# One bias buffer for both halves of a convolution, and three projection panels one stage earlier, in a decoder layer

## The chip, the core and the metric

The kernel runs on one core of a Trainium2 chip. A core has four engines that compute and take their work from queues of their own: TensorE (PE) multiplies matrices into PSUM, VectorE (DVE) and ScalarE (ACT) work elementwise, GpSimd (POOL) does small things. SyncE (SP) issues nearly all DMAs here. What counts is the device time of one execution, in microseconds (us). The inputs, weights and intermediate results that don't fit lie in DRAM.

## What is computed

One layer of a decoder on 1024 tokens of width 1024: a mixer made of a convolution group and a recurrent group, cross-attention into 256 memory tokens, and a gated feed-forward; each with a norm before and after, and a residual. Cut to what matters here:

```python
h = rms_norm(x, g[0])
p = h @ w_in_first                                  # 1024 columns for the convolution, 1792 for the recurrence
y_conv = conformer_conv(p[..., :2 * D_CONV], ...)
y_rwkv, _ = rwkv7_mix(p[..., 2 * D_CONV:], ...)
x = x + rms_norm(jnp.concatenate([y_conv, y_rwkv], -1) @ w_out, g[1])
x = x + rms_norm(memory_cross_attention(rms_norm(x, g[2]), ...), g[3])
x = x + rms_norm(swiglu(rms_norm(x, g[4]), ...), g[5])

def conformer_conv(u, conv_w, conv_b, ln_g, ln_b):
    h = u[..., :D_CONV] * sigmoid(u[..., D_CONV:])
    h = depthwise_causal_conv(h, conv_w) + conv_b   # 31 taps on each of 512 channels
    return silu(layer_norm(h, ln_g, ln_b))
```

## The kernel before

**Halves.** The sequence is worked off in two halves of 512 tokens (`b` is 0 or 1). Everything of half 1 up to its recurrence depends on half 0 only through small state, so that work of both halves can run side by side.

**Projections.** A matrix product in float32 is made of three with split operands: `split` writes a rounded copy (`hi`, on ACT) and the rest (`lo`, on DVE); `mm3` multiplies three pairs. `wload` loads 512 KB of weights (`wraw`, four buffers) and splits them into `whi` and `wlo` (two buffers each). `feat` is one projection of 128 columns for 512 tokens: 24 matmuls into `psf`. `w_in_block` runs panels, pairs of such projections; the input projection has 22 of them for each half: 8 for the convolution (`conv_cols`, stored in `hd`) and 14 for the recurrence (`mix_cols`, seven panels, stored in `pdr`; `evq` and `carry` are their evacuation on DVE).

**The convolution.** `conv_taps` loads 128 channels (`hin`), starts the sum with an ACT operation that multiplies by the first tap and adds the bias, and adds 30 taps on DVE (`acc`); 4 groups of channels make 120 taps for a half. `conv_norm` sums the groups (`lnsa`, `lnsb`), lets PE sum over channels with a matrix of ones (`psln`), and goes through squares, a reciprocal square root, and a SiLU whose two ACT operations read scale and bias. The result goes to DRAM (`yd`).

**The stages around the change.** While the recurrence of half 0 (`rwkv_chain`, tiles `Sn`, `Y`, `psp` to `psy`) runs, `weave` interleaves the memory products and the convolution projections of half 1 (`main`) with the convolution of half 0 in the program. The rest of half 1's input projection is a `filler`: 14 projections that `fill` takes a few at a time wherever the program has a gap. Then `mix_out(0)` loads `yd` (`araw`), splits it and multiplies with `w_out` into `pst`; `residual` adds and norms four token tiles (`ya`) and PE transposes them (`pstr`); `attention(0)` multiplies with `gd`, does a softmax and multiplies with `vwd`, then a second `residual`. The convolution of half 1 (`conv(1, kp)`) is woven into these two. Behind them come the feed-forward of half 0, as filler for the recurrence of half 1, and then half 1's own stages.

**Order.** The program order is not the order on the engines: when the program is built, a scheduler that estimates times puts every instruction in its engine's queue as soon as its inputs and buffers allow. Buffers (`bufs`) thus decide what may run ahead. Inside a queue the order is fixed.

## Time and profile before

| | us |
|---|---|
| median of 3 runs | 1670.16 (1668.98 to 1670.85) |
| the profiled execution | 1666.79 |
| its span, first to last instruction | 1665.1 |
| PE busy in it | 1513.3 |
| DVE busy in it | 1068.6 |
| ACT busy in it | 686.9 |

A profile lists what each engine did in one execution. Busy time as a share of the span tells which engine is full on average; windows tell it for a stretch; the list of waits tells for whom an engine stood still; the timeline gives each instruction with its start. Matmuls overlap, so that their own durations are longer than the step from one to the next.

### The profile page before, as it was taken

The page shows a single profiled execution, that of the slowest core. Times are in us where ns is not written, and L with a number is a line of the kernel's source. Part 1 is how long each engine was busy: PE and PEld are TensorE (multiplying, and loading weights), DVE is VectorE, ACT ScalarE, POOL GpSimd, SP SyncE. Part 2 cuts the span into 40 slices and gives each one's busy share as a digit, 9 for nine tenths or more (in the row PEclk, how much of TensorE's full clock was granted, in tenths as well). Part 3 has the DMA queues.
Part 4 walks back from the last instruction along what each step waited for, and adds up shares of the span by engine and source line. Part 5 has one row for each costly group of instructions (what it writes and reads, how often), then busy time and mean ns, then how long its engine had stood idle before and what let it go on. Part 6 is the DMA issues. An engine that isn't in the chain of part 4 may idle for free.

```text
span 1665.1 us, 22614 instructions
## 1 busy us (share of the span) xinstructions
PE 1513.3 (91%) x8688; PEld 1239.4 (74%) x8688; DVE 1068.6 (64%) x1702; ACT 686.9 (41%) x1062; POOL 50.8 (3%) x102
## 2 busy tenths in 40 slices
PE   7999879995009899999999999999999999999997
PEld 6787768874007688878788877888888788888886
DVE  5678676899998745568868355556446734444345
ACT  5654455543133634465522343444334432222222
POOL 1000100000000100100000000001001100000000
PEclk9999889998559999999999999999999999999999
DMA  5577996763014722645685544356226732332321
GB/s 206 170 223 213 310 304 191 240 201 101 6 35 155 253 76 95 201 141 174 181 230 189 153 149 148 111 167 210 81 89 203 252 102 89 101 101 89 102 89 51
DMA packets 175643, 257.36 MB, mean 155 GB/s; under 512 B 68912, under 2 KB 110000, under 8 KB 175536
## 3 DMA queue, kind: packets, MB, share of 16 engines
q1 hardware_dynamic: 174576, 255.08, 48.2%
q8 instruction: 68, 1.11, 0.3%
q10 hardware_dynamic: 960, 0.85, 0.2%
q14 instruction: 39, 0.32, 0.1%
HBM read 196.58 MB, written 59.31 MB: 154 GB/s over the span
## 4 chain that ended last, share of the span: by engine, by line
PE 81%; DVE 11%; DMA 4%; ACT 3%; issue 1%; SPq 0%; POOL 0%; DVEq 0%; POOLq 0%; ACTq 0%
PE psf L190 14%; PE psf L192 14%; PE psf L191 14%; PE pst L190 10%; PE pst L191 10%; PE pst L192 10%; DVE acc L342 6%; PE psg L514 1%; DVE wlo L168 1%; PE pstr L270 1%; PE pspr L428 1%; DMA gd<-evg 1%; ACT whi L167 1%; DMA xt<-in_x_dram 1%; DMA hin<-hd 1%
## 5 line engine op out<-in xcount | busy, mean ns | idle before, releaser
L168 DVE TENSOR_TENSOR wlo<-wraw,whi 128x1024 fp32r<-128x1024 f32 x256 | 312.8, 1223 | 321.7 <-ACT whi L167 319.7
L167 ACT CAST whi<-wraw 128x1024 fp32r<-128x1024 f32 x256 | 268.2, 1049 | 548.8 <-PE psf L191 228.7
L190 PE MATMUL psf<-ahi,whi 128*128 128x512 f32 (+1 forms) x1200 | 455.6, 381 | 3.2 <-ACT whi L167 3.0
L192 PE MATMUL psf<-ahi,wlo 128*128 128x512 f32 (+1 forms) x1200 | 454.9, 380 | 2.1 <-DVE wlo L168 2.1
L191 PE MATMUL psf<-alo,whi 128*128 128x512 f32 (+1 forms) x1200 | 454.7, 379 | 0.0
L190 PEld LDWEIGHTS psf<-ahi,whi 128*128 128x128 f32 x1200 | 227.7, 190 | 47.2 <-ACT whi L167 4.8
L192 PEld LDWEIGHTS psf<-ahi,wlo 128*128 128x128 f32 x1200 | 227.5, 190 | 44.9 <-DVE wlo L168 3.0
L191 PEld LDWEIGHTS psf<-alo,whi 128*128 128x128 f32 x1200 | 227.8, 190 | 42.3 <-issue 1.2
L342 DVE SCALAR_TENSOR_TENSOR acc<-hin,cols,acc 128x512 f32<-128x512 f32 x240 | 166.9, 746 | 4.0 <-ACT acc L340 3.8
L190 PE MATMUL pst<-whi,ahi 128*128 128x512 f32 x384 | 138.6, 400 | 22.7 <-ACT ahi L167 21.6
L191 PE MATMUL pst<-wlo,ahi 128*128 128x512 f32 x384 | 150.7, 394 | 0.0
L192 PE MATMUL pst<-whi,alo 128*128 128x512 f32 x384 | 147.3, 394 | 0.0
L191 PE MATMUL pst<-wlo,fhi 128*128 128x512 f32 x352 | 137.9, 392 | 0.0
L190 PE MATMUL pst<-whi,fhi 128*128 128x512 f32 x352 | 134.2, 392 | 0.0
L192 PE MATMUL pst<-whi,flo 128*128 128x512 f32 x352 | 134.1, 390 | 0.0
L190 PEld LDWEIGHTS pst<-whi,ahi 128*128 128x128 f32 x384 | 72.7, 191 | 40.1 <-ACT ahi L167 23.1
L191 PEld LDWEIGHTS pst<-wlo,ahi 128*128 128x128 f32 x384 | 73.1, 190 | 14.9
L192 PEld LDWEIGHTS pst<-whi,alo 128*128 128x128 f32 x384 | 72.2, 189 | 15.1 <-DVE alo L168 0.2
L903 DVE TENSOR_TENSOR ya<-pst,ya 128x512 f32<-128x512 f32 x80 | 54.2, 688 | 43.7 <-PE pst L192 43.5
L921 DVE SCALAR_TENSOR_TENSOR ftg<-ftg,psf 128x512 f32<-128x512 f32 x44 | 30.2, 685 | 76.4 <-PE psf L192 76.1
L191 PEld LDWEIGHTS pst<-wlo,fhi 128*128 128x128 f32 x352 | 66.1, 188 | 14.2 <-DVE wlo L168 0.4
L192 PEld LDWEIGHTS pst<-whi,flo 128*128 128x128 f32 x352 | 66.1, 188 | 13.6
(236 smaller groups left out, 1664.3 us busy)
## 6 DMA issues: line engine op xcount, KB each, us to landing
wraw<-in_w_gu_dram SPq DMA_DIRECT2D x88, 512.0 KB, 3.6
wraw<-in_w_in_dram SPq DMA_DIRECT2D x44, 512.0 KB, 4.1
wraw<-in_w_down_dram SPq DMA_DIRECT2D x44, 512.0 KB, 3.5
wraw<-in_wkv_dram SPq DMA_DIRECT2D x16, 512.0 KB, 5.7
am<-amd SPq DMA_DIRECT2D x16, 512.0 KB, 4.4
wraw<-in_w_out_dram SPq DMA_DIRECT2D x16, 512.0 KB, 3.7
wraw<-gd SPq DMA_DIRECT2D x16, 512.0 KB, 4.5
wraw<-vwd SPq DMA_DIRECT2D x16, 512.0 KB, 3.3
```

The source lines that it names most:

```text
L167: self.nc.scalar.copy(out=hi, in_=src)
L168: self.nc.vector.tensor_tensor(out=lo, in0=src, in1=hi.bitcast(F32), op=ALU.subtract)
L190: mm(ps, w[0], x[0], start=start, stop=False)
L191: mm(ps, w[0], x[1], start=False, stop=False)
L192: mm(ps, w[1], x[0], start=False, stop=stop)
L270: nc.tensor.transpose(ps[:, t * P:(t + 1) * P], xt[:, k * P:(k + 1) * P], self.ident)
L342: nc.vector.scalar_tensor_tensor(out=a, in0=h[:, k:k + TB], scalar=w(k), in1=a, op0=ALU.mult, op1=ALU.add)
L428: nc.tensor.matmul(ps, w, x, start=i == 0, stop=i == len(terms) - 1)
L514: nc.tensor.matmul(pg[g][:, i, :], bk[half[g], c + i, :], aq[half[g], :, c + i, :], start=True, stop=True)
L903: nc.vector.tensor_tensor(out=y, in0=ps, in1=y, op=ALU.add)
L921: nc.vector.scalar_tensor_tensor(out=tg, in0=tg, scalar=0.5, in1=pu, op0=ALU.mult, op1=ALU.mult)
```

## The change

Two things. First, the biases: the convolution bias (4 columns) and the layer norm's halved bias (4 columns) are copied into one tile `cb` of 8 columns, tag `convb`, which has one buffer. Half 0 reads the tile made at the start. When `conv_taps` begins for half 1, it allocates the tile anew in the same buffer and fills it with two ACT copies, which must wait until the last reader of half 0 has finished; all of half 1's sums start from it. A spare tile shrinks from 40 to 32 columns to make room. Second, the first three of the seven `mix_cols` panels of half 1 run in the `main` part of the recurrence's stage, and four are left to the filler; an empty `islice(w1, 0)` goes.

```diff
@@ -122,7 +122,7 @@
         nc.gpsimd.memset(self.mhalf, -0.5)
         self.carry = cp.tile([P, 14], F32, name="carry")
         nc.gpsimd.memset(self.carry, 0.0)
-        pad = cp.tile([P, 40], F32, name="pad")
+        pad = cp.tile([P, 32], F32, name="pad")
         nc.gpsimd.memset(pad, 0.0)
 
         def derive(name, n, src, mul, add):
@@ -139,6 +139,9 @@
         nc.vector.tensor_scalar(self.cwh, self.cwh, 0.5, None, op0=ALU.mult)
         self.lgh = derive("lgh", 4, col("ln_g"), 0.5, 0.0)
         self.lbh = derive("lbh", 4, col("ln_b"), 0.5, 0.0)
+        self.cb = cp.tile([P, 8], F32, tag="convb", name="convb0")
+        nc.vector.tensor_copy(out=self.cb[:, 0:4], in_=col("conv_b"))
+        nc.vector.tensor_copy(out=self.cb[:, 4:8], in_=self.lbh)
 
         self.hd = dr.tile([DR, CONVW - 1 + SEQ], F32, name="hd")
         self.pdr = dr.tile([14 * P, SEQ], F32, name="pdr")
@@ -331,13 +334,18 @@
 
     def conv_taps(self, b, pool, acc):
         nc = self.nc
+
+        if b == 1:
+            self.cb = self.cp.tile([P, 8], F32, tag="convb", name="convb")
+            nc.scalar.copy(out=self.cb[:, 0:4], in_=self.col("conv_b"))
+            nc.scalar.copy(out=self.cb[:, 4:8], in_=self.lbh)
         t0 = b * TB
         for j in range(4):
             h = pool.tile([P, 576], F32, tag="hin", bufs=2, name="hin")[:, 0:TB + CONVW - 1]
             nc.sync.dma_start(out=h, in_=self.hd[j * P:(j + 1) * P, t0:t0 + TB + CONVW - 1])
             a = acc[:, j, :]
             w = lambda k: self.cwh[:, j * CONVW + k:j * CONVW + k + 1]
-            nc.scalar.activation(out=a, in_=h[:, 0:TB], func=AF.Identity, scale=w(0), bias=self.col("conv_b", j))
+            nc.scalar.activation(out=a, in_=h[:, 0:TB], func=AF.Identity, scale=w(0), bias=self.cb[:, j:j + 1])
             for k in range(1, CONVW):
                 nc.vector.scalar_tensor_tensor(out=a, in0=h[:, k:k + TB], scalar=w(k), in1=a,
                                                op0=ALU.mult, op1=ALU.add)
@@ -377,7 +385,7 @@
             a = acc[:, j, :]
             nc.vector.tensor_tensor(out=a, in0=a, in1=ry, op=ALU.mult)
             th = pool.tile([P, TB], F32, tag="t", bufs=2, name="lnth")
-            sc, bi = self.lgh[:, j:j + 1], self.lbh[:, j:j + 1]
+            sc, bi = self.lgh[:, j:j + 1], self.cb[:, 4 + j:5 + j]
             nc.scalar.activation(out=th, in_=a, func=AF.Tanh, scale=sc, bias=bi)
             nc.scalar.activation(out=a, in_=a, func=AF.Identity, scale=sc, bias=bi)
             nc.vector.scalar_tensor_tensor(out=a, in0=th, scalar=1.0, in1=a, op0=ALU.add, op1=ALU.mult)
@@ -997,10 +1005,11 @@
                 yield 1.0 * 2
         maps = self.memory_maps(mT, ev, kv)
         w1 = self.w_in_block(1, h1, ev, conv_cols)
-        main = chain(islice(maps, 16), next_norm(), islice(w1, 0), maps, w1)
+        w1m = self.w_in_block(1, h1, ev, mix_cols[:3])
+        main = chain(islice(maps, 16), next_norm(), maps, w1, w1m)
         drain(weave(main, self.conv(0, kp), 1.0))
         pop("mix0", "gn0", "conv0", "tt0", "xb", "kv", "mk")
-        self.filler = self.w_in_block(1, h1, ev, mix_cols)
+        self.filler = self.w_in_block(1, h1, ev, mix_cols[3:])
 
         yp = push("y0", L)
         a2 = push("a2", L)
```

The engines' queues are built anew from that. Three places show it.

DVE in the recurrence's stage of half 0, before (`acc_2696` is half 0's sum, `acc_4446` half 1's, `Sn` the recurrence's state):

```order
L342 SCALAR_TENSOR_TENSOR acc_2696<-hin_3553,cols_77,acc_2696 128x512
L342 SCALAR_TENSOR_TENSOR acc_4446<-hin_4766,cols_77,acc_4446 128x512
L342 SCALAR_TENSOR_TENSOR acc_2696<-hin_3212,cols_77,acc_2696 128x512
L342 SCALAR_TENSOR_TENSOR acc_4446<-hin_4447,cols_77,acc_4446 128x512
L342 SCALAR_TENSOR_TENSOR acc_2696<-hin_3553,cols_77,acc_2696 128x512
L342 SCALAR_TENSOR_TENSOR acc_4446<-hin_4766,cols_77,acc_4446 128x512
L688 TENSOR_TENSOR Sn_2544<-pss_2535,Sn_2480 128x256
L342 SCALAR_TENSOR_TENSOR acc_2696<-hin_3212,cols_77,acc_2696 128x512
```

DVE at the same place, after (`acc_2699` is half 0's sum, `psf` and `evh` belong to half 1's convolution projections):

```order
L350 SCALAR_TENSOR_TENSOR acc_2699<-hin_3215,cols_77,acc_2699 128x512
L350 SCALAR_TENSOR_TENSOR acc_2699<-hin_3556,cols_77,acc_2699 128x512
L350 SCALAR_TENSOR_TENSOR acc_2699<-hin_3215,cols_77,acc_2699 128x512
L325 SCALAR_TENSOR_TENSOR evh_4307<-tg_4240,psf_4282 128x512
L350 SCALAR_TENSOR_TENSOR acc_2699<-hin_3556,cols_77,acc_2699 128x512
L350 SCALAR_TENSOR_TENSOR acc_2699<-hin_3215,cols_77,acc_2699 128x512
L171 TENSOR_TENSOR wlo_4351<-wraw_4348,whi_4350 128x1024
L696 TENSOR_TENSOR Sn_2547<-pss_2538,Sn_2483 128x256
L350 SCALAR_TENSOR_TENSOR acc_2699<-hin_3556,cols_77,acc_2699 128x512
L708 TENSOR_TENSOR Y_2561<-psy_2552,yq_2525 128x4x64
```

The taps of half 1 are gone from here; its first one now stands behind half 0's last step.

PE in front of the output projection, before (`psp` to `psbs` are the recurrence's last step, `pst` the output projection):

```order
L681 MATMUL psu_2605<-pt_2583,TT_1480 64x64 x8
L686 MATMUL pss_2616<-uv_2499,bt_2497 64x64
L696 MATMUL psy_2628<-am_2495,uv_2499 64x64
L686 MATMUL pss_2616<-uv_2499,bt_2497 64x64 x7
L696 MATMUL psy_2628<-am_2495,uv_2499 64x64 x7
L404 MATMUL psbs_2647<-yhl_2644,blk_105 128x512
L405 MATMUL psbs_2647<-yhl_2644,blk_105 128x512
L357 MATMUL psln_3824<-lnsa_3819,ones_86 128x512
L370 MATMUL psln2_3914<-lnsq_3911,ones_86 128x512
L190 MATMUL pst_4466<-whi_4472,ahi_4331 128x512
```

PE at the same place, after (`psf_4640` is the eighth of the 14 projections):

```order
L193 MATMUL psf_4640<-ahi_199,whi_4636 128x512
L194 MATMUL psf_4640<-alo_200,whi_4636 128x512
L195 MATMUL psf_4640<-ahi_199,wlo_4637 128x512
L365 MATMUL psln_3827<-lnsa_3822,ones_86 128x512
L378 MATMUL psln2_3917<-lnsq_3914,ones_86 128x512
L193 MATMUL pst_4694<-whi_4700,ahi_4559 128x512
```

Two of the 14 projections stood ahead of `psln` before; now eight do, and the recurrence's last step has moved ahead, among them.

DVE at the end of half 0's first residual, before (`ya_4458` and `ya_4459` are the third and fourth token tile, `evq` a projection's evacuation, `lnth` the end of half 1's convolution):

```order
L256 TENSOR_SCALAR ya_4458<-ya_4458,rstd_4899 128x1024
L304 SCALAR_TENSOR_TENSOR evq_4934<-psf_4909,cols_77,evq_4934 128x511
L307 SCALAR_TENSOR_TENSOR evq_4934<-carry_111,cols_77,evq_4934 128x1
L754 SCALAR_TENSOR_TENSOR ya_4459<-ya_4459,rstd_4942,xres_4940 128x1024
L383 SCALAR_TENSOR_TENSOR acc_4446<-lnth_6229,acc_4446 128x512
L309 COPY carry_111<-psf_4909 128x1
L229 TENSOR_SCALAR rstd_4950<-ss_4948 128x1
L168 TENSOR_TENSOR wlo_5106<-wraw_5103,whi_5105 128x1024
L304 SCALAR_TENSOR_TENSOR evq_4985<-psf_4960,cols_77,evq_4985 128x511
L307 SCALAR_TENSOR_TENSOR evq_4985<-carry_111,cols_77,evq_4985 128x1
L256 TENSOR_SCALAR ya_4459<-ya_4459,rstd_4950 128x1024
```

DVE at the same place, after (`ya_4686` and `ya_4687` are the third and fourth tile, `acc_4671` half 1's sum):

```order
L350 SCALAR_TENSOR_TENSOR acc_4671<-hin_5664,cols_77,acc_4671 128x512
L259 TENSOR_SCALAR ya_4686<-ya_4686,rstd_5127 128x1024
L350 SCALAR_TENSOR_TENSOR acc_4671<-hin_5467,cols_77,acc_4671 128x512
L762 SCALAR_TENSOR_TENSOR ya_4687<-ya_4687,rstd_5170,xres_5168 128x1024
L350 SCALAR_TENSOR_TENSOR acc_4671<-hin_5664,cols_77,acc_4671 128x512
L350 SCALAR_TENSOR_TENSOR acc_4671<-hin_5467,cols_77,acc_4671 128x512
L350 SCALAR_TENSOR_TENSOR acc_4671<-hin_5664,cols_77,acc_4671 128x512
L232 TENSOR_SCALAR rstd_5178<-ss_5176 128x1
L350 SCALAR_TENSOR_TENSOR acc_4671<-hin_5467,cols_77,acc_4671 128x512
L350 SCALAR_TENSOR_TENSOR acc_4671<-hin_5664,cols_77,acc_4671 128x512
L259 TENSOR_SCALAR ya_4687<-ya_4687,rstd_5178 128x1024
```

Before, half 1's taps were all ahead of this; now they stand between the steps of the tiles, by turns on two groups.

PE at half 0's second residual, before (`psf_6017` is the third of seven projections there, `pstr` the transposes of the first tile):

```order
L190 MATMUL psf_6017<-ahi_182,whi_6013 128x512
L191 MATMUL psf_6017<-alo_183,whi_6013 128x512
L270 MATMUL pstr_6172<-ident_81,ya_5560 128x128
L270 MATMUL pstr_6179<-ident_81,ya_5560 128x128
L270 MATMUL pstr_6186<-ident_81,ya_5560 128x128
L192 MATMUL psf_6017<-ahi_182,wlo_6014 128x512
```

PE at the same place, after (`psf_6157` is the only projection there):

```order
L194 MATMUL psf_6157<-alo_200,whi_6153 128x512
L195 MATMUL psf_6157<-ahi_199,wlo_6154 128x512
L273 MATMUL pstr_6252<-ident_81,ya_5788 128x128
L273 MATMUL pstr_6259<-ident_81,ya_5788 128x128
L273 MATMUL pstr_6266<-ident_81,ya_5788 128x128
```

Behind the transposes now follow the feed-forward's projections, which need their result; no other projection is left for this place.

## Rows read from the trace of the kernel before

**Rows 1.** the page's parts 1 and 2, shares of the span, and busy tenths by slice

```profile
PE 1513.3 (91%) x8688; PEld 1239.4 (74%) x8688; DVE 1068.6 (64%) x1702; ACT 686.9 (41%) x1062; POOL 50.8 (3%) x102
...
PE   7999879995009899999999999999999999999997
...
DVE  5678676899998745568868355556446734444345
```

**Rows 2.** windows: us, then busy us of PE, PEld, DVE, ACT, POOL, PEclk, DMA share, GB/s

```profile
400.00:501.00 101.00, 9.86 (x70) 5.41 (x70) 100.96 (x158) 22.05 (x31) 0.00 (x0) 0.52 0.10 34
501.00:560.00 59.00, 58.49 (x243) 47.36 (x244) 48.23 (x74) 29.23 (x49) 1.92 (x3) 0.95 0.52 173
560.00:580.00 20.00, 13.71 (x64) 10.90 (x63) 15.82 (x32) 12.99 (x20) 3.66 (x5) 0.88 0.84 311
...
680.00:728.00 48.00, 48.00 (x229) 39.87 (x228) 29.98 (x53) 21.86 (x33) 4.53 (x8) 1.00 0.65 202
```

**Rows 3.** waits of PE from 340 to 510: who waited for whom, us, times, longest

```profile
PE psln L357 <- DVE lnsa L351: 49.2, 1, 49.2
...
PE pst L190 <- ACT ahi L167: 21.6, 1, 21.6
```

**Rows 4.** timeline of DVE, 355 to 500: start, us, line, operation, tiles, count

```profile
356.52 0.68 DVE L351 TENSOR_TENSOR lnsa<-acc 128x512 f32<-128x512 f32 x1
...
396.99 1.21 DVE L168 TENSOR_TENSOR wlo<-wraw,whi 128x1024 fp32r<-128x1024 f32 x1
...
398.78 0.74 DVE L304 SCALAR_TENSOR_TENSOR evq<-psf,cols,evq 128x511 f32<-128x511 f32 x1
...
437.83 25.26 DVE L342 SCALAR_TENSOR_TENSOR acc<-hin,cols,acc 128x512 f32<-128x512 f32 x38
463.01 0.69 DVE L351 TENSOR_TENSOR lnsb<-acc 128x512 f32<-128x512 f32 x1
...
470.64 1.40 DVE L342 SCALAR_TENSOR_TENSOR acc<-hin,cols,acc 128x512 f32<-128x512 f32 x2
471.97 0.68 DVE L351 TENSOR_TENSOR lnsq<-lnsq 128x512 f32<-128x512 f32 x1
...
497.76 0.68 DVE L383 SCALAR_TENSOR_TENSOR acc<-lnth,acc 128x512 f32<-128x512 f32 x1
```

**Rows 5.** groups of DVE by line, 356 to 498.5: busy us, mean ns, idle before

```profile
L342 DVE SCALAR_TENSOR_TENSOR acc<-hin,cols,acc 128x512 f32<-128x512 f32 x154 | 105.9, 745 | 1.8 <-ACT acc L340 1.8
```

**Rows 6.** timeline of PE, 392 to 510

```profile
392.25 0.39 PE L192 MATMUL psf<-ahi,wlo 128*128 128x512 f32 x1
...
501.51 0.79 PE L190 MATMUL pst<-whi,ahi 128*128 128x512 f32 x1 [21.55 <-ACT ahi L167]
...
506.77 0.39 PE L190 MATMUL pst<-whi,ahi 128*128 128x512 f32 x1
```

**Rows 7.** the chain that ended last, around 354

```profile
353.63 5.14 DMA hin<-hd
```

**Rows 8.** timeline of ACT, 350 to 362

```profile
358.80 0.82 ACT L340 ACTIVATE acc<-hin,cols 128x512 f32<-128x512 f32 x1 [2.16 <-DMA hin<-hd]
```

**Rows 9.** timeline of PE at half 0's first residual

```profile
578.39 0.90 PE L270 MATMUL pstr<-ident,ya 128*128 128x128 f32 x3 [5.94 <-DVE ya L256]
579.64 0.80 PE L190 MATMUL pst<-whi,ahi 128*128 128x512 f32 x1 [0.35 <-ACT ahi L273]
```

**Rows 10.** timeline of DVE at half 0's second residual

```profile
678.72 1.27 DVE L754 SCALAR_TENSOR_TENSOR ya<-ya,rstd,xres 128x1024 f32<-128x1024 f32 x1
...
699.94 0.75 DVE L256 TENSOR_SCALAR ya<-ya,rstd 128x1024 f32<-128x1024 f32 x1 [0.60 <-POOL rstd L230]
```

**Rows 11.** timeline of PE at half 0's second residual

```profile
679.17 0.39 PE L192 MATMUL pst<-whi,alo 128*128 128x512 f32 x1
...
684.61 0.39 PE L192 MATMUL psf<-ahi,wlo 128*128 128x512 f32 x1
...
722.14 1.03 PE L270 MATMUL pstr<-ident,ya 128*128 128x128 f32 x8
```

## The prediction

> **What bounds the kernel now.** I read the busy tenths of the 40 slices first [rows 1]. TensorE (PE) is full nearly everywhere except in slices 10 to 12, and exactly there VectorE (DVE) is full. The windows give the sizes [rows 2]: from 400 to 501 us PE works 9.9 of 101 us at a granted clock of 0.52 (close to its lower level, 1.2 GHz) while DVE works 100.96. Behind it PE has no gap worth naming, but for 6.3 us in 560 to 580. So the kernel is PE-bound with one hole of about 100 us. The list of waits names what ends the hole [rows 3]: PE stands 49.2 us for `lnsa`, the sum over half 0's convolution, and 21.6 us for the first split input of the output projection, which reads that convolution's result.
>
> The timeline of DVE shows why half 0 is so late [rows 4]. Between `lnsa` at 356.5 and `lnsb` at 463.0 lie 106.5 us without a gap but 1.8 us [rows 5]. The order of before shows what runs there: 60 taps of half 0 and 59 of half 1, by turns. Half 1's result isn't read until the output projection of half 1, far behind; it takes the DVE time that half 0 needs at once.
>
> **Part 1, half 1 waits.** Both halves now read their biases from one buffer. Half 1's copy into it can't start before half 0's last activation has read it, and half 1's taps need that copy. The order of after has no tap of half 1 ahead of half 0's last step. A tap costs 25.26/38 = 0.665 us [rows 4]. Of the 106.5 us, 119 taps are 79.1 and all else 27.4. Without half 1: 60 taps, 39.9, and the 27.4. To this come six more projections (part 2). Each takes DVE a split of 1.21, an evacuation of 0.74 and two one-column steps; starts follow one another closer than the durations say (0.745 lasts a tap that takes 0.665 of the queue), so I take 2.0 a projection, 12.0 in all. The sum is 79.3, so `lnsb` starts at 356.5 + 79.3 = 435.8 in place of 463.0. PE doesn't set this end: it finishes its part of before at 392.6 [rows 6], the six projections add 32.7 (part 2), which makes 425.3, and the recurrence's small matmuls leave it some ten us of room.
>
> From `lnsb` to the output projection's first matmul were 38.5 us (463.0 to 501.51). Seven steps of that chain wait for one or two taps of half 1 in front of them, as the add at 471.97 does for the two taps at 470.64 [rows 4]; at about 1.2 each that is 8.2, which goes. It leaves 30.3, and the output projection starts at 466.1: **35.4 us earlier**. The layer norm's own latency stays bare, since DVE has nothing else queued in front of it now. The two bias copies on ScalarE (ACT) are 128x4, so between nothing and the 0.82 us of a 128x512 activation [rows 8] each; they stand behind half 0's last activation and cost half 0 nothing. The two at the start of the program hide behind the first loads.
>
> **Part 2, six projections move.** A projection is 24 matmuls; at full clock, 2.4 GHz, 24 in a row take 684.61 - 679.17 = 5.44 us [rows 11]. Before, two of the fourteen ran ahead of the hole's end; after, eight do. The six take 32.7 us of PE time out of the stretch behind, where PE is full (48.0 of 48 in 680 to 728 [rows 2]), and put them into the hole. Their loads, evacuations and stores go along on SP, ACT and DVE; ACT is busy 22 of 101 us there and the DMA share is 0.10. Parts 1 and 2 could give 35.4 + 32.7 = **68.1 us**, if nothing new were late.
>
> **Part 3, what is new at the first residual.** Now 120 taps, 79.8 us, must run beside the output projection and the first attention product, where 27 were left before. DVE was busy 48.2 of 59 us there [rows 2]. While the output projection runs this fits: its order puts 5 or 6 taps between two splits, 6 x 0.665 + 1.21 = 5.2 us, and PE needs 5.44 for what a split feeds. But the residual adds and scalings of the four token tiles stand between taps. From the first tap to the fourth scaling the order has 72 taps (47.9), 12 splits (13.7), 16 halves of 0.6 (9.6), 4 adds of 1.2, 4 scalings of 0.67, 4 evacuations with their columns (3.4) and small things: 84 us. The first tap starts near 463.3 (before, half 0's last step ended at 498.4 [rows 4], 3.1 us ahead of the projection's start). In the middle the last two groups' input must be loaded, with DVE waiting for it: such a load took 5.1 us and its activation 0.8 [rows 7, 8], and DVE has about 4.5 us of other work between the last tap on a group and the first on the next, so over both I add 3. The fourth scaling ends at 550.3, and the attention product follows 1.3 later [rows 9], at 551.6. That is 85.5 us after the output projection's start, against 579.64 - 501.51 = 78.1 before; the 5.9 us of waiting [rows 9] become 13 to 14. **Loss 7.4**, and 2 more for splits inside the product that come out a microsecond late. If DVE runs freely the loss is 0; if every tap in the way counts, see the rivals.
>
> **Part 4, the second residual loses its cover.** Before, seven projections ran between the last attention matmul at 679.17 and the last transposes at 722.14 [rows 11], 43.6 us without a gap. After, only one does, then PE waits for the four tiles. Their chain took from 678.72 to 699.94 plus 0.75 [rows 10], paced by the projections' own splits; the new order lets tiles three and four overlap, so I take 17 us from the last matmul. One projection covers 5.4, so PE waits 11.6; a restart at the lower clock costs 2.5 (12 matmuls took 506.77 - 501.51 = 5.26 [rows 6], at full clock half of 5.44), feeding the first projection 2, transposes 3.5 as before. Sum 25 for 43.6: of the 32.7 us only 18.2 arrive. **Loss 14.5.** If the chain were no shorter than before, 4 us more are lost; fully hidden, nothing.
>
> **Sum.** 68.1 - 7.4 - 2 - 14.5 = 44. The profiled execution took 1666.8, with a span of 1665.1; it would take 1623. The median of the runs is 3.4 above it, so I predict 1670.2 - 44 = **1626 us**.
>
> **Rivals.** *Everything is covered.* The taps let the residuals through and the feed-forward matmuls fill the second one: 68 off, 1602. For it: PE has always other matmuls in the program. Against: the order of PE puts the transposes ahead of them. *Only the panels count.* Something else ends the hole at 501 (the recurrence's output, also read by the projection): 18 off, 1652. Against: its last DVE step stands ahead of half 0's last taps in both orders. *Slower: the displaced taps land on PE's path.* DVE takes its work in order, so a split that PE needs waits for the taps queued ahead of it. 120 - 27 = 93 taps are displaced, 61.8 us; with all of it on the path, 35.4 + 18.2 - 61.8 = -8.2, 1678. It decides where more than (5.44 - 1.21)/0.665 = 6.4 taps stand between two splits. Against: at most 6 do in the output projection; for it: 23 do at the first residual. The Trainium skill ("TensorE: Matmul & The Clock Gate", section on the array's architectural detail) calls the queues of ACT and DVE strictly first in, first out; by that rule alone this rival is open wherever taps lead. The trace agrees: PE's 49.2 us wait [rows 3] passed while DVE worked off taps of a result nobody waited for. *No change.* PE's work isn't cut, so a kernel whose PE is busy 91% of the span [rows 1] could stay at 1670. The Trainium skill ("Perfetto Trace Analysis", "Identifying the Most-Contended Engine") says to work on the engine with the highest occupancy first, which here would be PE and not this hole. The trace speaks against it in this stretch: there the full engine is DVE [rows 2].
>
> **How the numbers follow.** Forecast 76%, spread 1612 to 1642 (the loss of parts 3 and 4 between 10 and 40, and 5 for part 1); all covered 12%; only panels 5%; slower 5%; no change 2%. The range 1605 to 1652 takes in the forecast's spread, about half of the first rival's and the second. A measurement of this kernel can tell about 0.2%, 3.3 us, from no change: faster 0.93, same 0.02, slower 0.05.
>
> **What would show it.** `lnsb` of half 0 near 436 and the output projection near 466; no tap of half 1 ahead of 460; eight projections before the hole, now 30 to 40 us long and still at the lower clock; a PE gap of 12 to 18 us at the first residual with taps on DVE, and a new one of 10 to 15 us at the second; behind it the same spans as before. It is wrong if `lnsb` stays beyond 450 (PE or loads hold the projections), if the gap at the first residual exceeds 25 us, or if splits in the output projection make PE wait.

## The result, and the profile after

The changed kernel takes 1639.12 us (median of 4 runs, 1638.08 to 1640.46) against 1669.57 before: a ratio of 0.982, 95% interval 0.9803 to 0.9837. The profiled execution's span went from 1665.1 to 1637.8 us. Forecast were 1626 and 44 us; 30 came.

The page of the changed kernel (parts 1 and 2) answers to [rows 1]: the hole in slices 10 to 12 is now a dip to 6 and 5 tenths in slices 11 and 12, and new dips stand behind it, in slices 14, 15 and 17.

```profile
PE 1521.8 (93%) x8688; PEld 1240.5 (76%) x8688; DVE 1066.9 (65%) x1704; ACT 685.9 (42%) x1064; POOL 54.6 (3%) x102
...
PE   7999878999659789699999999999999999999997
...
DVE  5687675999879996686775455637537634344445
```

The windows (columns as in [rows 2]) show the same in us: up to the output projection at 468, to the first attention product at 553, through attention to its last matmul, and to the feed-forward's first full stretch. The last line is attention in the kernel before.

```profile
400.00:468.00 68.00, 35.02 (x164) 25.81 (x162) 54.06 (x92) 30.77 (x42) 0.00 (x0) 0.75 0.34 111
468.00:553.00 85.00, 70.25 (x300) 56.59 (x300) 81.45 (x131) 30.79 (x51) 7.55 (x8) 0.92 0.58 187
553.27:662.25 108.98, 104.42 (x464) 84.69 (x464) 87.75 (x154) 50.27 (x95) 0.55 (x1) 0.97 0.29 89
662.00:706.00 44.00, 29.86 (x122) 21.54 (x121) 26.47 (x41) 24.41 (x39) 4.11 (x8) 0.82 0.42 141
```

```profile
579.64:679.17 99.53, 99.53 (x459) 82.41 (x460) 47.13 (x87) 38.22 (x78) 0.55 (x1) 0.99 0.27 88
```

DVE is now full through the first residual (81.5 of 85 us) and busy for 87.8 of 109 us in attention, where 47.1 of 99.5 were busy before. The list of TensorE's waits from 400 to 720 answers to [rows 3]:

```profile
PE pstr L273 <- DVE ya L259: 23.6, 5, 6.8
PE pst L193 <- ACT ahi L170: 17.1, 1, 17.1
PE psln L365 <- DVE lnsa L359: 10.3, 1, 10.3
PE psln L378 <- DVE lnsq L359: 5.9, 1, 5.9
PE psf L193 <- ACT pb L872: 2.1, 1, 2.1
PE pst L193 <- ACT pb L872: 2.1, 1, 2.1
```

The 49.2 us for `lnsa` are 10.3. In their place stand 23.6 us for `ya`, five times, where there was one of 5.9 [rows 9], and two of 2.1 each for `pb`, the softmax's output, in attention. The timeline of DVE, for [rows 4]: between the two sums lie 82.6 us and not 106.5, and the first tap of half 1 starts at 464.56.

```profile
357.10 0.68 DVE L359 TENSOR_TENSOR lnsa<-acc 128x512 f32<-128x512 f32 x1
...
439.71 0.69 DVE L359 TENSOR_TENSOR lnsb<-acc 128x512 f32<-128x512 f32 x1
...
464.56 4.11 DVE L350 SCALAR_TENSOR_TENSOR acc<-hin,cols,acc 128x512 f32<-128x512 f32 x6 [0.38 <-ACT acc L348]
```

The timeline of PE gives the places that the prediction named, for [rows 6, 9, 11]: the output projection, the last tiles' transposes and the first attention product, the last attention matmul, and the waits of the second residual's tiles.

```profile
468.35 0.80 PE L193 MATMUL pst<-whi,ahi 128*128 128x512 f32 x1 [17.08 <-ACT ahi L170]
...
546.12 0.90 PE L273 MATMUL pstr<-ident,ya 128*128 128x128 f32 x3 [6.76 <-DVE ya L259]
552.01 0.90 PE L273 MATMUL pstr<-ident,ya 128*128 128x128 f32 x3 [4.99 <-DVE ya L259]
553.27 0.79 PE L193 MATMUL pst<-whi,ahi 128*128 128x512 f32 x1 [0.35 <-ACT ahi L276]
...
662.25 0.39 PE L195 MATMUL pst<-whi,alo 128*128 128x512 f32 x1
...
673.06 0.90 PE L273 MATMUL pstr<-ident,ya 128*128 128x128 f32 x3 [4.65 <-DVE ya L259]
678.87 0.90 PE L273 MATMUL pstr<-ident,ya 128*128 128x128 f32 x3 [4.91 <-DVE ya L259]
682.04 0.90 PE L273 MATMUL pstr<-ident,ya 128*128 128x128 f32 x3 [2.27 <-DVE ya L259]
```

So the lead over the kernel before is 33.2 us at the output projection (501.51 to 468.35), 26.4 at the first attention product (579.64 to 553.27), 16.9 at the last attention matmul (679.17 to 662.25), and 27.3 at the end. Six projections, 32.7 us, were moved ahead of all this and should show as lead behind the last attention matmul; only 27.3 - 16.9 = 10.4 do.

### The profile page after: what moved, and what is told of

It reads as the page before. It is cut to its first block, busy times and chain, and to the rows that moved or that the text cites. A ratio compares the mean times of both kernels' runs of the same rounds, so it can differ in the third digit from the quotient of the medians.

```text
span 1637.8 us, 22612 instructions
## 1 busy us (share of the span) xinstructions
PE 1521.8 (93%) x8688; PEld 1240.5 (76%) x8688; DVE 1066.9 (65%) x1704; ACT 685.9 (42%) x1064; POOL 54.6 (3%) x102
## 4 chain that ended last, share of the span: by engine, by line
PE 85%; DVE 5%; DMA 4%; ACT 4%; issue 1%; SPq 0%; POOL 0%; DVEq 0%; POOLq 0%; ACTq 0%
PE psf L193 15%; PE psf L195 15%; PE psf L194 15%; PE pst L193 10%; PE pst L194 10%; PE pst L195 10%; PE psg L522 2%; DVE acc L350 1%; PE pstr L273 1%; PE pspr L436 1%; DVE wlo L171 1%; ACT whi L170 1%; DMA xt<-in_x_dram 1%; DVE ya L762 1%; PE psq L684 1%
## 5 line engine op out<-in xcount | busy, mean ns | idle before, releaser
L350 DVE SCALAR_TENSOR_TENSOR acc<-hin,cols,acc 128x512 f32<-128x512 f32 x240 | 170.7, 743 | 5.2 <-ACT acc L348 4.9
L195 PE MATMUL pst<-whi,flo 128*128 128x512 f32 x352 | 134.0, 390 | 0.0
L193 PEld LDWEIGHTS pst<-whi,ahi 128*128 128x128 f32 x384 | 72.9, 191 | 40.2 <-ACT ahi L170 18.6
L233 POOL TENSOR_TENSOR rstd<-rstd,mhalf 128x1 f32<-128x1 f32 x50 | 37.2, 753 | 1319.0 <-DVE rstd L232 1319.0
```

Source lines behind the costliest of these rows:

```text
L193: mm(ps, w[0], x[0], start=start, stop=False)
L195: mm(ps, w[1], x[0], start=False, stop=stop)
L233: nc.gpsimd.tensor_tensor(r, r, self.mhalf, op=ALU.pow)
L350: nc.vector.scalar_tensor_tensor(out=a, in0=h[:, k:k + TB], scalar=w(k), in1=a, op0=ALU.mult, op1=ALU.add)
```

## The experiments

The theory at this point, the ledger: 33.2 + 32.7 were won; 6.8 went at the first residual, 9.5 in attention, 22.3 behind it. The rivals: that the gain comes from the panels, and that the losses in attention and behind it have other causes than the order. The table has, for each kernel, the start of the output projection, three durations (output projection to first attention product; attention, first to last matmul; from there to the first `ftg`, the feed-forward's first result on DVE) from its trace, and its median in us. The medians were timed in groups, each beside the kernel before, whose own median lay between 1666.8 and 1669.6; the ratios in the text are to that. Each trace is one execution, so that a start can lie some us off for reasons ahead of the edit.

| | output projection | to attention | attention | to `ftg` | median |
|---|---|---|---|---|---|
| before | 501.5 | 78.1 | 99.5 | 52.9 | 1669.6 |
| changed kernel | 468.4 | 84.9 | 109.0 | 43.2 | 1639.1 |
| hold alone | 455.7 | 81.9 | 110.7 | 52.8 | 1635.0 |
| panels alone | 511.9 | 77.4 | 100.1 | 44.1 | 1670.6 |
| two panels | 467.6 | 81.4 | 111.1 | 45.8 | 1637.1 |
| taps late | 477.8 | 70.3 | 98.8 | 44.0 | 1684.5 |
| taps in the recurrence | 463.8 | 70.2 | 98.8 | 53.7 | 1680.0 |
| taps from the inverse | 456.4 | 70.4 | 98.6 | 52.9 | 1643.9 |
| taps in two parts | 453.9 | 80.4 | 100.8 | 52.9 | 1654.0 |
| feed-forward first | 468.4 | 84.0 | 109.6 | 39.0 | 1660.1 |
| the same, count kept | 468.8 | 84.7 | 108.3 | 40.0 | 1635.8 |

**The hold alone, and the panels alone.** Two kernels that each do one part.

```diff
-        w1m = self.w_in_block(1, h1, ev, mix_cols[:3])
+        w1m = self.w_in_block(1, h1, ev, mix_cols[:0])
-        self.filler = self.w_in_block(1, h1, ev, mix_cols[3:])
+        self.filler = self.w_in_block(1, h1, ev, mix_cols)
```

> The hold alone: the shared bias tile stays, all seven panels go back to the filler. Ledger theory, read from the trace of the changed kernel (lead 33.2 at the output projection, 26.4 at the first attention product, 16.9 at its end, so 6.8 lost at the first residual and 9.5 in attention; 22.3 of the 32.7 us of moved projections lost from the second residual on): without six projections in the hole the convolution of half 0 has 12 us less DVE work in front of it, lnsb starts at 425 to 428 in place of 439.7, the output projection at 454 to 457; 45 to 47 earlier than before, less 6.8 and 9.5, and nothing lost at the second residual, which has its seven projections back: 1638 to 1642, the same as with the panels. The sum as predicted (attention loses 2, not 9.5): 1632. Rival, that the panels carry the gain and the hold little: above 1650.

```diff
-        if b == 1:
-            self.cb = self.cp.tile([P, 8], F32, tag="convb", name="convb")
-            nc.scalar.copy(out=self.cb[:, 0:4], in_=self.col("conv_b"))
-            nc.scalar.copy(out=self.cb[:, 4:8], in_=self.lbh)
```

> The panels alone: six projections move into the mixers' stage, half 1 doesn't wait for half 0's biases. Ledger theory: the taps of both halves run by turns again, with 12 us more DVE work in the hole; lnsb starts near 475, the output projection near 513, 12 later than before; 32.7 us of projections are out of the way behind it, and 22 of them are lost again at the second residual and the start of the feed-forward: 32.7 - 12 - 22 = -1, so 1666 to 1674, no change. With the predicted loss of 14.5 there: 1663. Rival, that the panels carry the gain: 1652 or less.

The hold alone took 1634.99 us, ratio 0.9794 (0.978 to 0.9809): `lnsb` at 426.99, output projection at 455.65, both where the ledger had them, and the total is 4 us below the changed kernel, just below the 1638 to 1642 of the ledger and above the 1632 of the prediction's sum. Its ledger closes: a lead of 45.9 us at the output projection, 3.8 lost on the way to attention, 11.1 in attention and nothing behind leave 31.0; the span is 30.6 shorter. Its waits of TensorE from 400 to 720:

```profile
PE psln L365 <- DVE lnsa L359: 20.4, 1, 20.4
...
PE pstr L273 <- DVE ya L259: 10.8, 2, 5.8
```

At the first residual two waits remain, at the second none. The panels alone took 1670.62, ratio 1.0012 (1.0001 to 1.0023): no change, as expected. Its waits from 400 to 760:

```profile
PE psln L361 <- DVE lnsa L355: 48.2, 1, 48.2
PE pst L193 <- ACT ahi L170: 21.6, 1, 21.6
PE pstr L273 <- DVE ya L259: 17.0, 4, 5.1
```

The hole is as before (48.2), and three tiles of the second residual and one of the first are now waited for (17.0). So the whole gain is the hold's, and the panels are worth nothing without it. With it they seem to cost 3 to 4 us (spans 1637.8 and 1634.5); every run of the hold alone is faster than every run of the changed kernel, but they were timed in different groups, and the intervals of the ratios, 0.9803 to 0.9837 and 0.978 to 0.9809, just overlap. The table shows how: against the hold alone the changed kernel starts the output projection 12.7 us later (439.71 - 426.99 = 12.7 for `lnsb`), and of the 32.7 us moved, 52.8 - 43.2 = 9.6 arrive behind attention.

**Two panels in place of three.**

```diff
-        w1m = self.w_in_block(1, h1, ev, mix_cols[:3])
+        w1m = self.w_in_block(1, h1, ev, mix_cols[:2])
-        self.filler = self.w_in_block(1, h1, ev, mix_cols[3:])
+        self.filler = self.w_in_block(1, h1, ev, mix_cols[2:])
```

> As the changed kernel, but two panels move in place of three, so that three projections in place of one cover the second residual. Ledger theory: output projection 4 us earlier (464), 21.8 us of projections moved, 6.8 and 9.5 lost as before, and at the second residual 16.3 us of cover for four tiles whose chain takes about 17, so no more than 5 to 10 lost: 37 + 21.8 - 16.3 - (5 to 10) = 32 to 38, 1632 to 1637, faster than three panels. Rival, that each moved projection loses the same share (22.3 of 6, 3.7 each): 1642, slower than three panels.

1637.10, ratio 0.9814 (0.98 to 0.9829): just beyond the expected 1632 to 1637 and between none (1635.0) and three (1639.1), though the intervals of neighbours overlap. In the trace the output projection didn't come 4 us earlier (467.6), but that execution (1640.73) is the slowest of this kernel, and its `lnsa` already came 3.2 later than in the changed kernel (360.32 for 357.10); from `lnsa` to `lnsb` it took 78.6 us for 82.6, the expected 4 less. Behind attention 52.8 - 45.8 = 7.0 of 21.8 us arrive, a third, as with three panels (9.6 of 32.7). So each moved projection loses about the same share, as the rival had it, though the rival's 1642 was too slow.

**Half 1's taps taken away from the residuals.** Two kernels move them by a longer hold (the bias copies add a zero made from a late value): behind the second residual, and, without panels, behind the first state of half 1's recurrence.

```diff
-            nc.scalar.copy(out=self.cb[:, 0:4], in_=self.col("conv_b"))
+            nc.scalar.activation(out=self.cb[:, 0:4], in_=self.col("conv_b"), func=AF.Identity, bias=self.zl)
...
+            self.zl = self.cp.tile([P, 1], F32, name="zl")
+            nc.vector.tensor_scalar(self.zl, ss[3][:, 1:2], 0.0, None, op0=ALU.mult)
...
+                nc.vector.tensor_scalar(self.zl, Sn[:, 0, 0:1], 0.0, None, op0=ALU.mult)
```

The second `tensor_scalar` is that of the other kernel.

> As the changed kernel, but half 1's convolution waits, through its bias, for half 0's second residual, and stands behind the preparation of half 1's recurrence in the program. Ledger theory, by which half 1's taps in DVE's queue cause the losses at the first residual and in attention: output projection still near 468, the first attention product near 546 (lead 33), the end of attention near 646 (lead 33), then the same 22 lost behind: 1623, and up to 10 more if the taps now delay the feed-forward's splits. Rival, that the attention's 9.5 have another cause (loads, the lower clock after the gap): the lead falls there by 7 to 10 again, 1632 or more.

> Hold alone (no panel moves), and half 1's convolution waits longer: through its bias for the first state of half 1's own recurrence, so that its 120 taps lie beside that recurrence and the feed-forward. Theory, that half 1's taps in DVE's queue cause the losses at the first residual (3.7 in the run with the hold alone) and in attention (11), and that the second residual loses nothing with its seven projections: output projection near 456, lead 46 kept through the first attention product (near 533), the end of attention (near 633) and to the end: 1622 to 1626. Rival, that the taps only move their damage: half 1's recurrence (states now 126 us from first to last) is stretched so far that the feed-forward runs out and TensorE waits ahead of half 1's output projection, as when the taps stood ahead of the recurrence: above 1640.

1684.51 (1.0093, 1.008 to 1.0106) and 1680.01 (1.0074, 1.0053 to 1.0094): far off as totals, while the disputed stretch is clear. Attention takes 98.8 us in both, as before the change (99.5), and the way to it 70.3, eight less than before. So half 1's convolution, beside which these stages ran, is what cost the 9.5 us in attention and the waits of the first residual. What both totals say is another thing: the work moved found no free place. With the taps ahead of the recurrence, half 1's first state came at 1029.8 (911.3 in the changed kernel), and from 1000 to 1100 TensorE stood for 30 of 100 us, at a mean granted clock of 0.74:

```profile
1000.00:1100.00 100.00, 69.50 (x991) 56.63 (x989) 48.67 (x89) 55.21 (x90) 0.00 (x0) 0.74 0.48 141
```

With the taps inside the recurrence, the sum of half 1 came after the feed-forward had run out, and TensorE waited for it ahead of half 1's output projection:

```profile
PE psln L365 <- DVE lnsa L359: 19.9, 1, 19.9
PE pst L193 <- ACT ahi L170: 17.8, 1, 17.8
```

Besides, both kernels have the slower projections of the last section, worth some 20 us in the run that has nothing else, and start the output projection later by 8 to 9 us. Without these 20 both would still be slower than the kernels that they start from.

**From the middle of the inverse.** The same hold, opened between these two places, and the slower projections avoided (`zl` in 8 columns taken from the spare tile).

```diff
+            if b == 1 and t == 15:
+                self.zl = self.cp.tile([P, 8], F32, name="zl")[:, 0:1]
+                nc.vector.tensor_scalar(self.zl, tm[:, 0, 0:1], 0.0, None, op0=ALU.mult)
```

> Hold alone, no panel moves, half 1's convolution waiting for the middle of the triangular inverse of half 1's recurrence, so that its taps lie beside the inverse's DMA latency and the recurrence, some 60 us earlier than in the run that waited for the first state; the tile that carries the wait has 8 columns, taken from the spare tile, so that nothing behind it moves by 4 bytes. Theory: the two residuals and attention keep the lead of 46 (out of 31 at the end of attention in the run with the hold alone), the feed-forward's matmuls start 0.2268 us apart again, and the convolution of half 1 is done near 1030, before TensorE runs out of feed-forward: 1620 to 1628. Rival, that recurrence and convolution together still end later than the feed-forward lasts (near 1045): a wait of TensorE ahead of half 1's output projection of 10 to 40 us, 1632 to 1660.

1643.90, ratio 0.985 (0.9834 to 0.9867). The windows from the output projection to attention and through it show what the two stages are without taps: TensorE is busy 69.4 of 71 and 98 of 98 us.

```profile
456.00:527.00 71.00, 69.39 (x301) 57.06 (x302) 36.83 (x58) 29.42 (x50) 4.60 (x8) 0.96 0.62 204
527.00:625.00 98.00, 98.00 (x458) 81.06 (x458) 47.45 (x90) 37.48 (x77) 0.55 (x1) 1.00 0.30 95
```

The lead at the end of attention is 679.17 - 625.37 = 53.8 us, more than the 46 expected. 21 of the span remain (1665.1 to 1644.0). The rival held: the loop of the inverse went from 813.5 to 913.2 (start of its first and of its last step), where it goes from 836.7 to 883.6 in the hold alone, the last state came at 1061.2 in place of 1043.2, and TensorE stood for 21 of the 50 us from 1030 on, with the granted clock at 0.66 on the mean:

```profile
1030.00:1080.00 50.00, 28.75 (x306) 22.77 (x305) 29.48 (x53) 28.72 (x44) 0.00 (x0) 0.66 0.42 131
```

**Half of the taps early, half late.** Two groups of channels as in the hold alone, two behind the inverse.

```diff
+                self.zl = self.cp.tile([P, 8], F32, name="zl")[:, 0:1]
+                nc.vector.tensor_scalar(self.zl, Tt[:, 0, 0:1], 0.0, None, op0=ALU.mult)
...
-        drain(weave(blocks(), self.conv(1, kp), 0.7))
+        drain(weave(blocks(), self.conv_taps(1, kp, ca, (0, 1)), 0.7))
```

> Hold alone, no panel moves, and half 1's convolution in two parts: two of its four groups of channels run as in the run with the hold alone (60 taps, beside the output projection and the first residual) and are stored; the other two wait for the end of the triangular inverse of half 1's recurrence, and so lie in the DMA latency between the inverse and the first state. Theory: 3.7 or less lost at the first residual (from a lead of 46), nothing in attention (the first attention matrix product to the end of attention in 98 to 99 us, not 108 to 110), nothing at the second residual, and a recurrence that starts early enough: 1622 to 1627, faster than the hold alone by 8 or more. Rival, that 60 taps ahead of half 1's first state still delay the recurrence past the end of the feed-forward, as 120 did: a wait ahead of half 1's output projection and 1630 to 1640.

1653.95, ratio 0.9912 (0.9897 to 0.9928): missed, and by a fault of the experiment. The value that opens the hold is one that the loop never writes again, so that it opened ahead of the loop, as the timeline of DVE shows; the taps then stood by turns with its steps, and it went from 823.6 to 943.0.

```profile
819.46 0.15 DVE L620 TENSOR_SCALAR zl<-Tt 128x1 f32<-128x1 f32 x1
823.56 0.19 DVE L616 TENSOR_TENSOR tm<-At,Tt 128x31 f32<-128x31 f32 x1 [3.96 <-issue]
...
838.09 0.75 DVE L355 SCALAR_TENSOR_TENSOR acc<-hin,cols,acc 128x512 f32<-128x512 f32 x1
838.75 0.35 DVE L617 TENSOR_TENSOR Tt<-Tt,tm 128x192 f32<-128x192 f32 x1
```

What it does tell: with 60 taps the way to attention takes nearly as long as in the hold alone (80.4 and 81.9, where it takes 70.2 to 70.4 without taps), and attention, without taps, is only some 2 us longer (100.8).

**Projections in the layer norm.** Two kernels let the loads of four or two more projections wait for `lnsb`, on top of the kernel with the taps in the recurrence.

```diff
+            if self.gated:
+                self.gated -= 1
+                if self.gated < 4:
+                    self.nc.gpsimd.tensor_copy(out=raw[:, 0, 0:1], in_=self.zg)
             self.nc.sync.dma_start(out=raw, in_=src.rearrange("p (k n) -> p k n", k=k))
```

> As the run before it, but four more of half 1's projections run ahead of the output projection, and their loads wait for the sum lnsb of half 0's convolution, so that they fall into its layer norm, where DVE has free time, and not into its taps. Theory: moved work is worth 5.44 a projection less what the second residual loses for lack of cover (9.5 for four, measured with two panels moved) and less 0 to 4 for splits in the layer norm's way: 21.8 - 9.5 - (0 to 4) = 8 to 12 faster than the run before it, 1611 to 1618. Rival, that the splits and loads delay the layer norm by 8 or more: no faster than the run before it.

> The same with two projections in place of four. Theory: 10.9 moved, the second residual keeps five projections, 27 us for a chain of about 17 to 25, and loses 0 to 4: 7 to 10 faster than without, 1613 to 1619, about the same as with four. Rival, that the loss is the same share for each moved projection: half the gain of four.

1673.45 (1.0038, 1.0025 to 1.0052) and 1676.68 (1.0049, 1.003 to 1.0068), 6.6 and 3.3 below their base: less than expected for both, and half the gain for half the projections, as the second one's rival had it. But it isn't shown that the moved projections made this gain: in both, `lnsa` already came earlier than in their base (360.1 and 363.8 for 365.6), ahead of anything that the gate holds, and these kernels have one more tile of one column, so that their data lie elsewhere again. With four, `lnsb` came at 427.94 and the output projection at 466.7, 38.8 later, where the changed kernel needs 28.6: the splits and evacuations stand in the layer norm's chain.

**The feed-forward's first weights ahead of the preparation.** In the changed kernel TensorE loses time once more around 700, behind the second residual. The timeline of ACT there:

```profile
698.36 1.28 ACT L239 ACT_TABLE_LOAD   x1 [4.13 <-DVE rn L468]
...
700.73 1.28 ACT L477 ACT_TABLE_LOAD   x1
...
702.61 1.04 ACT L170 CAST whi<-wraw 128x1024 fp32r<-128x1024 f32 x1
```

The split `whi` that the second matrix product of the feed-forward needs starts at 702.61, behind a square root of half 1's preparation and two table loads of 1.28 us. The edit issues four projections of the feed-forward first; a second kernel takes as many from the 270 us that follow half 1's recurrence.

```diff
+        self.fill(21.0)
         pp = push("prep1", R)
...
-        self.fill(270.0)
+        self.fill(249.0)
```

> As the changed kernel, but the program issues four projections of the feed-forward ahead of the preparation of half 1's recurrence, so that on ACT their weight splits stand in front of the preparation's square root and its table loads. Theory, that this order costs TensorE the 5.8 us after 698 (restart at the lower clock included): 1633 to 1636. Rival, that the weights' loads or the first projection's operands set that time: no change, 1637 to 1641.

> The run with four of the feed-forward's projections ahead of the preparation once more, but the same number are taken from what the program issues behind half 1's recurrence, so that the residuals of half 1 keep their cover. Theory: the 5 us won at the start of the feed-forward (its output sums then came 744.3 - 739.4 = 4.9 earlier) arrive at the end, and the waits of 5.3, 8.0, 7.3 and 3.8 us at half 1's residuals are gone: 1633 to 1636. Rival, that those waits come from the changed order and not from the missing cover: 1650 or more.

With the first line alone 1660.08 (0.9946, 0.9926 to 0.9965), a miss by 25 us, and yet the stretch behaved as expected. The timeline of ACT has the split at 698.71, ahead of the table load:

```profile
698.71 1.05 ACT L170 CAST whi<-wraw 128x1024 fp32r<-128x1024 f32 x1 [4.58 <-PE psf L194]
...
701.21 1.28 ACT L239 ACT_TABLE_LOAD   x1
```

The first `ftg` came at 700.9 in place of 705.5. The waits from 1100 to 1300 show where it was lost:

```profile
PE pstr L273 <- DVE ya L259: 17.1, 3, 8.0
PE pstr L273 <- DVE rstd L232: 7.3, 1, 7.3
```

These are half 1's residuals. Their cover is what is left of the feed-forward, and four projections of it had been used up earlier. With both lines: 1635.76, ratio 0.9798 (0.9782 to 0.9815), in the expected 1633 to 1636, 3.4 below the changed kernel's median. The medians are of different groups and their intervals overlap, but the stretch itself agrees: from the end of attention to the first `ftg` it is 3.2 us shorter (40.0 for 43.2). So some 3 of the 22.3 us behind attention are this order.

No version was clearly faster than the hold alone (1634.99) or this one (1635.76); the two don't differ measurably, and both are faster than the kernel before and lie below the changed one, with the reserve named for the hold alone.

## Why the prediction was right where it was

The range held the time and the sign was right; the size was 30 of 44. The hole was closed as forecast; what was sized too low is what the change costs in the stages behind it.

- **What bounds the kernel.** Right: the hole went with half 1's taps, and the hold alone gives all of the gain.
- **Part 1.** `lnsb` 439.7 for 435.8, output projection 468.35 for 466.1, 33.2 us for 35.4. Of the 3.9 us, 0.6 are `lnsa`, and 2.6 stand in the hold alone too (69.9 us between the sums for 67.3, the estimate less its 12 for the panels). From `lnsb` it took 28.6 for the estimated 30.3. The 12 us for the panels' work on DVE were 12.7 in the comparison with the hold alone, and 8.7 for 8 with two panels.
- **Part 2.** The six projections were moved as counted (6 x 5.44 is 32.6, not 32.7); TensorE's wait for the sum is 10.3, so that it did have the room.
- **Part 3.** 6.8 us for the 7.4 at the first residual: right, and TensorE waited 6.76 + 4.99 = 11.8 for the tiles, a little under the 13 to 14. One of the named signs of being wrong came, though small: one split in the output projection made TensorE wait (1.38 us for `wlo`, at 483.35). The 2 us "for splits inside the product" is the term that was mis-sized: attention lost 9.5. I costed the taps up to the fourth scaling and took the 48 behind it for harmless, because DVE has free time there on the mean. The timeline of DVE at the end of the first attention product shows what they do:

```profile
576.18 0.74 DVE L350 SCALAR_TENSOR_TENSOR acc<-hin,cols,acc 128x512 f32<-128x512 f32 x1
576.84 0.68 DVE L867 TENSOR_REDUCE mx<-pst 128x2 f32<-128x512 f32 x1
577.44 0.74 DVE L350 SCALAR_TENSOR_TENSOR acc<-hin,cols,acc 128x512 f32<-128x512 f32 x1
578.10 0.68 DVE L867 TENSOR_REDUCE mx<-pst 128x2 f32<-128x512 f32 x1
...
579.96 0.15 DVE L868 TENSOR_SCALAR mx<-mx 128x2 f32<-128x2 f32 x1
```

Each of the first three `mx`, the maximum that the softmax starts from, has a tap in front of it, so that the first is scaled only at 579.96. ACT's `pb` reads it, and TensorE, whose next matmuls need the buffers that the softmax frees, waits 2.06 us for `pb` at 581.40, and 2.1 once more 26 us later. The taps aren't alone in this wait: `mx` was ready at 580.1, but ACT had begun a weight split at 579.39 and started `pb` behind it, at 580.34. The kernels without half 1's convolution there take 98.6 to 98.8 us and have no such wait, which shows the cause as a whole. The traces divide the 9.5: TensorE works 104.4 of the 109.0 us, so 4.6 are waits. Of the 4.9 us that it works longer than before, 2.0 are the four `psln` matmuls of half 1's own layer norm, which ran ahead of attention before (half 1's `lnsb` came at 528.90 then and comes at 608.84 now):

```profile
L365 PE MATMUL psln<-lnsa,ones 128*128 128x512 f32 x2 | 1.0, 590 | 0.0
L378 PE MATMUL psln<-lnsq,ones 128*128 128x512 f32 x2 | 1.0, 590 | 0.0
```

The other 2.9 are the same matmuls taking longer, among other places behind the second wait, where the granted clock is below full:

```profile
609.00:615.00 6.00, 6.00 (x22) 4.78 (x22) 3.48 (x13) 2.12 (x9) 0.00 (x0) 0.79 0.30 87
```

The rule in the Trainium skill ("TensorE: Matmul & The Clock Gate", section on the array's architectural detail) that ACT and DVE work strictly in order holds here too, as the order of these DVE rows shows: it was the right one to apply past the first residual.

- **Part 4.** 22.3 for 14.5. The wait for the tiles was right (4.65 + 4.91 + 2.27 = 11.8 for 11.6). Missing was the second stall around 700: with no projections left between them, the feed-forward's start and half 1's preparation fall together on ACT, in an order that holds the feed-forward's weights back; undoing it gives 3.2 in that stretch and 3.4 in the total. The rest of the 7.8 that are missing, some 4 us, I can't assign. The sum has one restart at the lower clock; the windows show a granted clock of 0.50 from 673 to 683, 0.74 from 683 to 690 and 0.84 from 706 to 720, but no run isolates what that costs. The sum itself is off by a little: 43.6 - 25 leaves 18.6 and not 18.2.
- **Sum.** 33.2 + 32.7 - 6.8 - 9.5 - 22.3 = 27.3, the change of the span. The medians differ by 30.4, since the profiled execution of the changed kernel (1639.56) lies by its median and that of before (1666.79) below its own.
- **Rivals.** *Displaced taps on TensorE's path* was wrong as a total, but right as a mechanism for up to 16 of the 65.9 us (6.8 + 9.5). *Only the panels count* was wrong: they count for nothing alone. What the prediction didn't ask is whether part 2 pays at all: 32.7 moved, less 12 in the hole and 14.5 behind, was forecast at +6, and came out at -3 to -4. Behind the feed-forward's first result the two kernels take the same time, as the prediction had it (1665.1 - 732.0 = 933.1 and 1637.8 - 705.5 = 932.3).

## What to carry to other kernels

When a full engine makes another one stand, look first for work in its queue that nobody waits for yet; holding it back by one shared buffer gave some 34 us. Such work, and filler as well, has to lie somewhere: filler moved into one gap is missing in the next, and taps moved off one path landed on another in six of these kernels, so a move is to be summed over every stage up to where the orders agree again. Where an engine's queue is in order, a mean busy share of half says little; count what stands ahead of each instruction that another engine waits for.

## What the runs showed of the hardware that was not expected

**Four bytes.** The kernels with a new tile of one column (the late taps, those in the recurrence and the two built on these) had slower matmuls in all projections. One run tests it: the changed kernel with one number changed, the order of instructions on DVE and ACT the same.

```diff
-        pad = cp.tile([P, 32], F32, name="pad")
+        pad = cp.tile([P, 33], F32, name="pad")
```

> The changed kernel with one number changed: the spare tile has 33 columns in place of 32, so that what is allocated behind it lies 4 bytes further on; the order on every engine is the same. Theory, from the runs with a tile of one column, whose projections' matmuls start 2% further apart (400 rows of them in 136.7 us in place of 134.0) at the full granted clock: matmuls that read operands shifted by 4 bytes take longer, 15 to 30 us in all, 1654 to 1670. Rival, that those runs were slower for another reason (the chip, the other order): 1637 to 1641.

1659.30 us, ratio to before 0.9946 (0.9929 to 0.9964), where the changed kernel has 0.982: 20 us for 4 bytes. The groups of PE from 1420 to 1600 us, mean ns of one matmul, first in the changed kernel, then with 33 columns:

```profile
L193 PE MATMUL psf<-ahi,whi 128*128 128x512 f32 x169 | 65.7, 389 | 0.0
...
L193 PE MATMUL pst<-whi,fhi 128*128 128x512 f32 x96 | 37.3, 389 | 0.0
```

```profile
L193 PE MATMUL psf<-ahi,whi 128*128 128x512 f32 x176 | 69.6, 396 | 0.0
L193 PE MATMUL pst<-whi,fhi 128*128 128x512 f32 x84 | 32.7, 389 | 0.0
```

The matmuls that stream activations (`psf`) take 396 ns for 389 at the full granted clock. Their starts, where one follows another directly, lie 0.2333 us apart on the mean for 0.2267 (1300 to 1640 us), which is 3%; 400 of them with the `pst` matmuls in between span 136.7 us for 134.0, the 2% of the expectation. Those that stream weights (`pst`) are unchanged. A run has 3 x 1040 `psf` matmuls of 512 columns; by estimate, 0.0066 us on each make 20.6 us, about the whole difference. The two kernels with two tiles of one column have the same 0.2333. In the change the spare tile shrinks by just the 8 columns that the new one takes, so that what lies behind it stays in place; what a shift by 8 columns would have cost was not tried, and neither was which operand's address matters or by what modulus.
